# Two-layer diffusion backbone: modulation products with the weights stationary in fp32, and an opening that goes 256 features at a time

## The chip, the cores and the metric

The kernel runs on one core of a Trainium2 chip. The metric is the device time in microseconds (us) of one execution. The engines are named as the profile names them: PE is TensorE (matrix products), PEld its loading of stationary operands, DVE is VectorE, ACT is ScalarE, POOL is GpSimd, and SP issues nearly all transfers.

## What is computed

Two layers act on 1024 latent tokens and 256 context tokens of 1024 features, in fp32. Only the modulation (adaLN) and the opening of the first layer are touched:

```python
def adaln(cond, w_mod, b_mod):                 # w_mod: 1024 x 6144 per layer
    m = jnp.dot(jax.nn.silu(cond), w_mod) + b_mod
    return jnp.split(m[..., None, :], 6, axis=-1)
...
sh1, sc1, g1, sh2, sc2, g2 = adaln(c, w_mod[l], b_mod[l])
csh1, csc1, cg1, csh2, csc2, cg2 = adaln(c_ctx, w_mod[l], b_mod[l])
h = modulate(rms_norm(x, norm1_g[l]), sh1, sc1)
hc = modulate(rms_norm(xc, norm1_g[l]), csh1, csc1)
# ... input projection of h and hc, attention, pooling, convolution, output projection, feed-forward
```

So each layer multiplies two vectors, the conditions of latents and context, by a 1024 x 6144 matrix: 25 MB of weights a layer, for two rows of output. The first layer can't make its first normed tokens before it has two of the six parts, the scale and the shift (chunks 1 and 0).

## The kernel before

Activations lie with features on partitions, 128 features a tile, and tokens along the free axis in blocks of 512, 512 and 256. An exact product of fp32 operands is made of three fast ones: a weight is split into a high and a low part by `Stream.split_to` (ACT copies the high part, DVE or POOL subtracts it), an activation likewise, and `proj` and `proj2` issue hi x hi, hi x lo and lo x hi.

The order of the instructions is written by hand with the help of a forecast. `Clock` keeps a rough time for each engine; work beside the main flow stands in lanes (`lane`, `_step`, `adv`), and a lane's next piece goes out when the forecast says it is due. `fill` gives PE pieces of the lane "ada" before a wait that the forecast sees. Each engine then runs its own instructions in that order.

The modulation before (`adaln`, `adaln_end`): the conditions are the stationary operand, a tile of 128 x 4 (two conditions, high and low parts), and the weights are moving, 512 columns at a time. One half of a chunk is 8 tiles of 128 features; a tile is split on ACT and on POOL (first layer) or DVE (second layer's), and takes two products of 512 columns. The 4 x 512 result is copied by ACT, turned by four transposes into columns, and DVE adds the bias.

- Opening (`run`): the first block's x is loaded, squared on ACT and summed on POOL (`sq_acc`), then all 32 tiles of chunks 1 and 0 (`whole=True`: every other tile unsplit, as two fp32 passes). Only when both chunks are complete does `norm_h` make the first block, feature tile by feature tile (a DVE product, an ACT pass for the high part, a DVE pass for the low one), and `in_proj` multiplies it with the first four column tiles of the input projection (b0, a0, b1, a1). The second block's squares are made during the first block's norm.
- Chunks 2, 4, 3, 5 of the first layer are the lane "ada" beside the rest of the input projection (lower parts on POOL). DVE then has 62 passes of the depthwise convolution over 1009 to 1024 tokens (`taps`) and as many over the context; the pooling's product (`pool_mix`) waits for operands that DVE makes in the same queue.
- All six chunks of the second layer are the lane "ada" beside the first layer's feed-forward.

The sums of squares over the features are themselves products: `rnorm` takes 128 tokens of the squares as stationary fp32 operand and a column of ones (or four of groups) as the moving one.

Of the kernel before, what the change touches and what calls it, by code (L numbers as in the profile page):

```python
# [15 lines left out]
P = 128  # L16
# [14 lines left out]
# column tiles of the input projection, in the order in which they are packed  # L31
# [3 lines left out]
# per-layer parameter columns  # L35
# [13 lines left out]
# when each operation of an attention unit goes out, in the order of which the units' are merged  # L49
# [14 lines left out]
RAW = 10  # L64
SQ = [0, 2, 4, 6, 8, 8, 8, 8, 8]
# [15 lines left out]
class Block:  # L81
    """A run of tokens: its width, and per 128 features the two parts of an operand."""
# [5 lines left out]
class Unit:  # L88
    """128 queries of one head, among the context's tokens or the latents'."""
# [15 lines left out]
class Clock:  # L105
    """A rough forecast of when each engine and each tile is ready, for the order of emission alone."""
# [46 lines left out]
class Eng:  # L153
    """An engine whose instructions are also put to the forecast."""
# [41 lines left out]
class Kern:  # L196
# [57 lines left out]
    def fill(self, *aps):  # L254
        """Before PE has to wait: give it what lanes have for it."""
# [7 lines left out]
    def finish(self, *names):  # L263
        """Emit what is left of lanes now."""
# [6 lines left out]
    def mm(self, out, lhsT, rhs, start, stop):  # L271
        self.tc.nc.tensor.matmul(out, lhsT, rhs, start=start, stop=stop)  # L272
        n = rhs.free_size()
        self.clock.run("pe", n * (0.000422 if rhs.dtype == F32R else 0.00168), [out], [lhsT, rhs] + ([out] if start else []), 0.3)
# [17 lines left out]
    def part(self, shape=(512,), dtype=F32):  # L292
        """Of an operand that stays for the phase."""
# [26 lines left out]
    def split(self, hi, lo, src, lo_eng=None):  # L320
        """hi + lo == src, each of them exact for the tensor engine."""
# [3 lines left out]
    def split2(self, hi, lo, src):  # L325
        """The same on a lane."""
# [41 lines left out]
    def proj(self, hi, lo, blocks, outs, order=range(KD), last=None):  # L368
        """A weight tile's product with some blocks, side by side up to number last."""
# [14 lines left out]
    def proj2(self, ws, blk, outs):  # L384
        """Two tiles' products with one block."""
# [9 lines left out]
    def adaln_setup(self):  # L395
        nc = self.nc
        c4 = self.cp.tile([P, KD, 4], F32, name="cond_raw")
        c_in = self.cp.tile([P, KD, 2], F32, name="cond_in")
        nc.sync.dma_start(c_in, self.io["cond"])
        nc.vector.memset(c4, 0.0)  # L400
        self.S = self.cp.tile([P, KD, 4], F32R, name="cond_st")
        self.c4, c0 = c4, c4[:, :, 0:2]
        self.act(c0, c_in, AF.Silu)
        nc.scalar.copy(self.S[:, :, 0:2], c0)
        nc.vector.tensor_tensor(self.S[:, :, 2:4], c0, r32(self.S[:, :, 0:2]), ALU.subtract)
        self.M = {}

    def adaln(self, l, chunks, pace, ne=2, whole=False, **kw):
# [3 lines left out]
        st = Stream(self, self.mod_aps(l, chunks, ne), new=self.part if whole else self.half if ne == 1 else self.big, **kw)  # L412
        i, ready = 0, []
        for chunk in chunks:
            m = self.cp.tile([P, 2, 8], F32, name=self.name("mod"))
            for n in range(2):
                ps = self.pm.tile([P, 512], F32, tag="mod", name=self.name("mod")) if self.pm else self.bank2()
                for kk in range(KD // ne):
                    if whole:
                        while len(ready) < min(i + 4, len(st.aps)):  # L420
                            w, odd = st.get_raw(len(ready)), len(ready) % 2
                            ready.append((self.part((ne, 512), F32R), self.part((ne, 512), F32R)) if odd else (w, None))
                            if odd:
                                self.split(*ready[-1], w)
                        hi, lo = ready[i]
                    else:
                        hi, lo = st.get(i)
                        yield self.pe(hi, lo, lag=ADA_LAG)
                    i += 1
# [1182 lines left out]
```

## Time and profile before

| | |
|---|---|
| time, median of 3 runs | 3152.94 us (3152.34 to 3154.36) |
| span of the profiled execution | 3148.1 us, 4.8 us under the median |
| PE busy | 2957.6 us, 94% of the span |
| DVE, ACT, POOL busy | 1728.9, 1098.9, 1135.8 us |
| mean granted TensorE clock | 0.977 of full |

The profiled execution took its span and what lies around it; its own time was not listed apart, so the difference to the median, 4.8 us, stands for the start and end that the span leaves out. Times in the rows count from the span's start. A line L272 is the helper that issues every product, L277 the one for transposes, L165 the wrapper of all other instructions, so groups are told apart by their tiles: `mod` is the PSUM bank of the modulation and its result, `cond_st` and `cond_raw` are the conditions, `part` and `half` are small tiles of 512 columns, `big` of 1024, `dww` the convolution's weights, `ones` the column of ones, `bank` a PSUM bank.

### The profile page before, as it was taken

The numbers are of one execution on the slowest core, as the hardware profiler recorded it, in microseconds if no ns is written. First come the engines' busy times: TensorE is split into PE (matmuls) and PEld (weight loads), VectorE is DVE, ScalarE is ACT, GpSimd is POOL, SyncE is SP. The second block draws the span as 40 slices with busy tenths as digits, with TensorE's granted clock in tenths as the row PEclk, the third lists the DMA queues.
The fourth block names the chain that finished last, engine by engine and source line by source line (L and its number), as shares of the span: only waits on it lengthen the run. The fifth ranks groups of instructions, "written<-read, shape, count | busy, mean of one in ns | idle before, by whom it ended". The sixth has DMA issues, their size and how long they took to land.

```text
span 3148.1 us, 38069 instructions
## 1 busy us (share of the span) xinstructions
PE 2957.6 (94%) x14708; PEld 2408.0 (76%) x14708; DVE 1728.9 (55%) x2413; ACT 1098.9 (35%) x1892; POOL 1135.8 (36%) x914
## 2 busy tenths in 40 slices
PE   6868898999999999999999998899999999999999
PEld 2646677877777778888888877678877888888887
DVE  5998758985645454332333498869956222322223
ACT  5424536763423332222222233357744111111110
POOL 3655406871423223233332423318832212211221
PEclk9989898999999999999999999999999999999999
DMA  6324364326333232111111222283252111111111
GB/s 229 108 90 122 123 192 140 105 76 203 114 100 95 93 101 81 34 41 41 34 41 40 75 68 70 81 239 95 88 173 75 48 47 54 47 47 47 48 47 54
DMA packets 133188, 283.52 MB, mean 90 GB/s; under 512 B 13840, under 2 KB 47248, under 8 KB 133008
## 3 DMA queue, kind: packets, MB, share of 16 engines
q1 hardware_dynamic: 132720, 280.83, 28.3%
q8 instruction: 116, 1.90, 0.3%
q14 instruction: 64, 0.52, 0.1%
q10 hardware_dynamic: 288, 0.26, 0.0%
HBM read 231.75 MB, written 49.28 MB: 89 GB/s over the span
## 4 chain that ended last, share of the span: by engine, by line
PE 61%; DVE 8%; issue 2%; ACT 1%; POOL 1%; DMA 1%; SPq 0%; DVEq 0%; ACTq 0%; POOLq 0%
PE bank L272 59%; DVE big L165 4%; DVE st L165 2%; DVE half L165 1%; PE S L272 1%; PE bank L277 1%; DVE part L165 1%; DVE at L165 1%; ACT p L165 0%; ACT big L165 0%; POOL p L165 0%; DMA big<-QS 0%; POOL big L165 0%; ACT half L165 0%; DVE rn L165 0%
## 5 line engine op out<-in xcount | busy, mean ns | idle before, releaser
L272 PE MATMUL bank<-part,big 128*128 128x512 f32 (+1 forms) x7536 | 1625.7, 374 | 29.8 <-DVE part L165 9.0
L272 PEld LDWEIGHTS bank<-part,big 128*128 128x128 f32 x7536 | 1321.6, 191 | 310.3 <-DVE part L165 12.9
L165 POOL TENSOR_TENSOR big<-big,big 128x1024 fp32r<-128x1024 f32 (+2 forms) x177 | 431.7, 2450 | 1141.5 <-ACT big L165 850.0
L272 PE MATMUL bank<-half,big 128*128 128x512 f32 (+1 forms) x2640 | 564.5, 373 | 5.4 <-DVE big L165 2.1
L272 PEld LDWEIGHTS bank<-half,big 128*128 128x128 f32 x2640 | 460.0, 188 | 104.4 <-DVE big L165 4.5
L165 DVE TENSOR_TENSOR big<-big,bank 128x512 f32<-128x512 f32 (+1 forms) x130 | 82.7, 679 | 821.4 <-PE bank L272 450.2
L165 DVE SCALAR_TENSOR_TENSOR big<-bank,mod,big 128x512 f32<-128x512 f32 (+1 forms) x560 | 390.4, 736 | 149.9 <-PE bank L272 143.6
L165 ACT CAST big<-big 128x1024 fp32r<-128x1024 f32 (+2 forms) x322 | 298.4, 955 | 68.8 <-DVE big L165 29.8
L165 POOL TENSOR_TENSOR half<-half,half 128x512 fp32r<-128x512 f32 (+2 forms) x141 | 202.7, 1445 | 328.7 <-ACT half L165 298.3
L165 DVE TENSOR_TENSOR big<-big,big 128x1024 fp32r<-128x1024 f32 (+3 forms) x177 | 214.8, 1220 | 188.1 <-ACT big L165 175.4
L165 ACT ACTIVATE big<-bank 128x512 f32<-128x512 f32 x88 | 48.1, 595 | 607.4 <-PE bank L272 607.4
L165 POOL TENSOR_TENSOR big<-big,half 128x256 f32<-128x256 f32 x160 | 124.7, 780 | 289.4 <-ACT half L165 289.4
L165 POOL TENSOR_TENSOR p<-p,p 128x512 f32<-128x512 f32 (+1 forms) x200 | 221.1, 1105 | 16.7
L165 ACT ACTIVATE half<-bank,mod 128x256 f32<-128x256 f32 x160 | 75.8, 474 | 375.1 <-PE bank L272 375.1
L165 DVE TENSOR_REDUCE st<-S 128x1 f32<-128x1280 f32 (+1 forms) x144 | 195.8, 1362 | 12.3 <-PE S L272 12.3
L165 DVE SCALAR_TENSOR_TENSOR big<-big,dww,big 128x1009 f32<-128x1009 f32 (+14 forms) x120 | 200.2, 1701 | 0.5
L165 POOL TENSOR_SCALAR p<-p,st 128x512 f32<-128x512 f32 (+1 forms) x200 | 123.3, 616 | 192.9 <-DVE st L165 150.7
L165 ACT ACTIVATE p<-S,st 128x1280 f32<-128x1280 f32 (+1 forms) x144 | 177.7, 1234 | 39.7 <-DVE st L165 38.0
L272 PE MATMUL S<-kv,big 128*128 128x512 f32 (+1 forms) x672 | 157.7, 370 | 9.6 <-ACT p L165 6.1
L272 PEld LDWEIGHTS S<-kv,big 128*128 128x128 f32 x672 | 120.1, 191 | 37.7 <-ACT p L165 12.3
L272 PE MATMUL bank<-at,kv 128*128 128x256 f32 x960 | 137.5, 290 | 0.0
L165 DVE TENSOR_TENSOR at<-bank,at 128x512 fp32r<-128x512 f32 (+1 forms) x200 | 115.7, 588 | 29.2 <-ACT at L165 25.0
(107 smaller groups left out, 2364.9 us busy)
## 6 DMA issues: line engine op xcount, KB each, us to landing
big<-in_w_ffn_in SPq DMA_DIRECT2D x88, 512.0 KB, 3.6
big<-in_w_mod SPq DMA_DIRECT2D x48, 512.0 KB, 3.8
big<-in_w_ffn_out SPq DMA_DIRECT2D x44, 512.0 KB, 3.7
big<-in_w_out SPq DMA_DIRECT2D x40, 512.0 KB, 4.9
half<-in_w_mod SPq DMA_DIRECT2D x64, 256.0 KB, 3.5
big<-QS SPq DMA_DIRECT2D x128, 128.0 KB, 5.3
big<-in_w_in SPq DMA_DIRECT2D x28, 512.0 KB, 4.8
VS<-big SPq DMA_DIRECT2D x40, 256.0 KB, 3.6
```

The costliest lines, as they stand in the source:

```text
L165: r = fn(*a, **k)
L272: self.tc.nc.tensor.matmul(out, lhsT, rhs, start=start, stop=stop)
L277: self.tc.nc.tensor.transpose(out, in_, ident)
```

## The change

The weights become the stationary operand, 128 x 128, in fp32 and unsplit, and the two conditions are two moving columns. An item is one chunk's 256 columns: four tiles of 256 rows by 256 columns, 16 products into 2 x 2 columns of PSUM, and DVE adds the bias from there. Copy, transposes and splits of the modulation are gone. The opening goes item by item, shift and scale of 256 features, then two feature tiles of the norm, then the first four column tiles' products with them; the first block's squares aren't summed on POOL any more but by PE (`rnorm` with a list). Comment lines that were taken out are not shown.

```diff
@@ mm
-        self.clock.run("pe", n * (0.000422 if rhs.dtype == F32R else 0.00168), [out], ...
+        self.clock.run("pe", n * 0.000422 if rhs.dtype == F32R else max(0.125, n * 0.00168), [out], ...
@@ rnorm
+        many = s if isinstance(s, list) else [s]
         for c in range(nb):
-            self.mm(ps[:, c * G:(c + 1) * G], s[:, c * P:(c + 1) * P], sel, True, True)
+            for i, x in enumerate(many):
+                self.mm(ps[:, c * G:(c + 1) * G], x[:, c * P:(c + 1) * P], sel, i == 0, i == len(many) - 1)
@@ adaLN
+    def adaln(self, l, items, pace, ne=2, new=None, now=False, raw_ahead=4):
+        st = Stream(self, self.mod_aps(l, items, ne), new=new or self.half, raw_ahead=raw_ahead)
+        n, i = KD // ne, 0
+        for chunk, c in items:
+            ws = []
+            for _ in range(n):
+                ws.append(st.get_raw(i))
+                i += 1
+            yield self.pe(*ws, lag=ADA_LAG)
+            ps = self.pm.tile([P, 512], F32, tag="mod", name=self.name("mod")) if self.pm else self.bank2()
+            for x in range(2):
+                for k in range(KD):
+                    self.mm(ps[:, 2 * x:2 * x + 2], ws[k // ne][:, k % ne, x * P:x * P + P], self.cond[:, k, :], k == 0, k == KD - 1)
+                if not now:
+                    yield pace / 2
+            end = self.adaln_end(l, chunk, c, ps)
+            if now:
+                for _ in end:
+                    pass
+            else:
+                self.lane("mod", end)
+            yield pace / 2
+
+    def adaln_end(self, l, chunk, c, ps):
+        yield self.at(ps)
...
+        nc.vector.tensor_tensor(part, ps[:, 0:4].rearrange("p (c j) -> p j c", j=2), bias, ALU.add)
         if chunk in (1, 4):
...
             nc.vector.scalar_tensor_tensor(part, part, 1.0, g, ALU.add, ALU.mult)
@@ in_proj
         for b in range(n):
+            if opened and b == 0:
+                for x, o in enumerate(opened[1]):
+                    gated(COLS[x], b, o)
+                continue
             self.finish(f"norm{b}")
@@ run
+        nc.sync.dma_start(self.params, io["params"])
+        ada = self.adaln(0, [(ch, c) for c in range(4) for ch in (1, 0)], 0.0, new=self.part, now=True, raw_ahead=4)
...
+        ada_step(1)
...
         for k in range(KD):
             nc.sync.dma_start(xs[k][0], io["xT"][k, :, 0:512])
+            sq.append(self.half())
+            self.act(sq[k], xs[k][0], AF.Square)
+        st_in = self.in_stream(0)
+        st_in.load_to(GATED)
...
+        ada_step(4)
         self.lane("norm0", norm_0())
+        self.finish("norm0")
...
+        ws = [st_in.get(x, 0) for x in range(GATED)]
+        outs = [self.bank() for _ in range(GATED)]
+        for c in range(4):
+            for _ in range(2 if c < 3 else 3):
+                next(norm0, None)
+            if c == 1:
+                for k in range(KD):
+                    nc.sync.dma_start(xs[k][1], io["xT"][k, :, 512:1024])
+            ada_step(4 if c < 3 else 1)
+            for k in range(max(0, 2 * c - 1), 2 * c + 1 if c < 3 else KD):
+                for (hi, lo), o in zip(ws, outs):
+                    self.mm(o, hi[:, k, :], lat[0].hi[k], k == 0, False)
+                    self.mm(o, hi[:, k, :], lat[0].lo[k], False, False)
+                    self.mm(o, lo[:, k, :], lat[0].hi[k], False, k == KD - 1)
...
+        for k in range(KD):
+            self.sq_acc(acc[1], xs[k][1], k == 0)
...
-        self.lane("ada", self.adaln(0, [2, 4, 3, 5], 3.0, ne=1, split_ahead=1, raw_ahead=1, lo=("p",)), ADA_AT)
+        self.lane("ada", self.adaln(0, [(ch, c) for ch in (2, 4, 3, 5) for c in range(4)], 6.0, raw_ahead=1), ADA_AT)
...
-            self.lane("ada", self.adaln(l + 1, [1, 0, 2, 4, 3, 5], 5.0, split_ahead=0, raw_ahead=1))
+            self.lane("ada", self.adaln(l + 1, [(ch, c) for ch in (1, 0, 2, 4, 3, 5) for c in range(4)], 20.0, ne=4, new=self.big, raw_ahead=1))
```

## Rows read from the trace of the kernel before

**Rows 1.** The profile's page: the span, busy time by engine, busy tenths of 40 slices with the granted clock, and the chain of work that ended last.

```profile
span 3148.1 us, 38069 instructions
...
PE 2957.6 (94%) x14708; PEld 2408.0 (76%) x14708; DVE 1728.9 (55%) x2413; ACT 1098.9 (35%) x1892; POOL 1135.8 (36%) x914
...
PE   6868898999999999999999998899999999999999
...
PEclk9989898999999999999999999999999999999999
...
PE 61%; DVE 8%; issue 2%; ACT 1%; POOL 1%; DMA 1%; SPq 0%; DVEq 0%; ACTq 0%; POOLq 0%
```

**Rows 2.** The view by windows, for the stages that hold modulation work and two that hold none (1240 to 1785 the rest of the feed-forward, 1785 to 2060 the second layer's norm and input projection).

```profile
core 0: us, PE busy (x) PEld busy (x) DVE busy (x) ACT busy (x) POOL busy (x), PEclk, DMA share, GB/s
104.00:391.00 287.00, 222.51 (x1079) 168.88 (x1078) 252.49 (x281) 111.35 (x214) 164.89 (x99) 0.88 0.36 118
...
840.00:1240.00 400.00, 397.74 (x2016) 314.53 (x2015) 196.87 (x259) 134.28 (x206) 110.47 (x82) 1.00 0.31 95
1240.00:1785.00 545.00, 545.00 (x2810) 462.92 (x2808) 186.06 (x288) 121.71 (x222) 170.10 (x143) 1.00 0.12 37
1785.00:2060.00 275.00, 239.19 (x1134) 195.44 (x1134) 237.14 (x296) 105.79 (x191) 89.91 (x48) 0.94 0.28 91
```

**Rows 3.** PE's groups of instructions by form: the modulation's products beside the feed-forward and in the first layer, its transposes, and the products with a column of ones, whose stationary operand is 128 x 128 fp32.

```profile
L272 PE MATMUL bank<-big,cond_st 128*4 128x512 f32 x192 | 52.9, 398 | 0.0
L272 PE MATMUL mod<-half,cond_st 128*4 128x512 f32 x128 | 45.6, 418 | 16.2 <-POOL half L165 13.3 <-ACT half L165 2.7
...
L277 PE MATMUL bank<-ident,half 4*128 4x4 f32 x96 | 9.9, 205 | 1.0 <-ACT half L165 0.7 <-ACT rn L165 0.4
L272 PE MATMUL bank<-ones,half 128*128 128x1 f32 x76 | 9.5, 244 | 2.7 <-POOL half L165 2.7
```

**Rows 4.** The timeline (start, length, count): eight records of the four products with ones of one norm at the full clock and what follows them; the loads of the last four such records of another norm at the half clock and what follows; four modulation products in the feed-forward and what follows.

```profile
19.25 0.95 PE L272 MATMUL bank<-ones,half 128*128 128x1 f32 x8
20.13 1.02 PE L272 MATMUL mod<-part,cond_raw 128*4 128x512 f32 x2
...
81.05 0.98 PEld L272 LDWEIGHTS bank<-ones,half 128*128 128x128 f32 x4
81.90 0.33 PEld L272 LDWEIGHTS bank<-part,big 128*128 128x128 f32 x1
...
1101.01 1.11 PE L272 MATMUL bank<-big,cond_st 128*4 128x512 f32 x4
1101.96 2.37 PE L272 MATMUL bank<-half,big 128*128 128x512 f32 x11
```

**Rows 5.** The view by windows (columns as in rows 2), at the start of the attention, where the products are short.

```profile
470.00:475.00 5.00, 4.85 (x20) 4.08 (x19) 2.88 (x10) 3.18 (x12) 2.46 (x5) 0.50 0.47 126
475.00:480.00 5.00, 4.79 (x20) 4.33 (x20) 3.39 (x13) 3.32 (x13) 1.88 (x3) 0.50 1.04 348
```

**Rows 6.** The timeline of the opening: a transfer's issue, first modulation product, POOL's sum of squares, transposes' end and the bias, the first block's first and last products, the second block's first, the end of that block's norm on DVE, and the first result of the second block that DVE takes for the convolution. Then the window of 15 to 29 us.

```profile
5.89 21.64 SPq L165 DMA_DIRECT2D part<-in_w_mod  x32
...
6.61 10.01 POOL L165 TENSOR_TENSOR half<-half,half 128x512 f32<-128x512 f32 x7 [5.31 <-ACT half L165]
...
11.72 1.86 PE L272 MATMUL mod<-part,cond_raw 128*4 128x512 f32 x2 [11.72 <-DMA part<-in_w_mod]
...
42.35 0.41 PE L277 MATMUL bank<-ident,half 4*128 4x4 f32 x4 [0.67 <-ACT half L165]
...
48.11 7.16 PE L272 MATMUL bank<-part,big 128*128 128x512 f32 x19 [5.36 <-ACT part L165]
...
73.75 3.18 PE L272 MATMUL bank<-part,big 128*128 128x512 f32 x13
...
81.97 5.28 PE L272 MATMUL bank<-part,big 128*128 128x512 f32 x12
...
96.78 1.62 DVE L165 SCALAR_TENSOR_TENSOR part<-half,mod,part 128x512 fp32r<-128x512 f32 x2
...
103.92 0.69 DVE L165 SCALAR_TENSOR_TENSOR big<-half,bank 128x512 f32<-128x512 f32 x1 [0.67 <-ACT half L165]
...
15.00:29.00 14.00, 12.86 (x46) 3.13 (x44) 7.25 (x16) 8.00 (x14) 1.61 (x1) 1.00 1.05 387
```

**Rows 7.** POOL's group of the modulation's lower parts from 80 to 391 us; a pass of the convolution by DVE between 104 and 182 us, beside POOL's work, and between 186 and 207 us, with POOL idle; PE's longest wait in the first 400 us (us in total, times, longest) and the product that ended it.

```profile
L165 POOL TENSOR_TENSOR half<-half,half 128x512 fp32r<-128x512 f32 x64 | 108.5, 1712 | 115.6 <-ACT half L165 89.2 <-DVE big L165 7.2 <-ACT rn L165 6.5
...
L165 DVE SCALAR_TENSOR_TENSOR big<-big,dww,big 128x1012 f32<-128x1012 f32 x2 | 4.5, 2240 | 0.0
...
L165 DVE SCALAR_TENSOR_TENSOR big<-big,dww,big 128x1022 f32<-128x1022 f32 x2 | 2.5, 1274 | 0.0
...
PE bank L272 <- DVE big L165: 37.1, 8, 25.8
...
208.97 1.22 PE L272 MATMUL bank<-big,pwr 128*128 128x512 f32 x2 [25.83 <-DVE big L165]
```

**Rows 8.** The timeline: one half chunk's transposes in the first layer, and DVE's reading of their result.

```profile
117.84 0.41 PE L277 MATMUL bank<-ident,half 4*128 4x4 f32 x4
...
127.75 0.15 DVE L165 TENSOR_TENSOR mod<-bank,params 128x8 f32<-128x8 f32 x1
```

More of the change, by code (lines that the diff above doesn't have):

```diff
@@ L63 @@
 P1_LO = ("v", "p", "v") + ("p",) * 11
-RAW = 10
-SQ = [0, 2, 4, 6, 8, 8, 8, 8, 8]
 FFN_LO = ("p",)
@@ L273, in mm @@
         n = rhs.free_size()
-        self.clock.run("pe", n * (0.000422 if rhs.dtype == F32R else 0.00168), [out], [lhsT, rhs] + ([out] if start else []), 0.3)
+        self.clock.run("pe", n * 0.000422 if rhs.dtype == F32R else max(0.125, n * 0.00168), [out], [lhsT, rhs] + ([out] if start else []), 0.3)
     def transpose(self, out, in_, ident):
@@ L406, in adaln_setup @@
-        self.M = {}
-    def adaln(self, l, chunks, pace, ne=2, whole=False, **kw):
-        nc = self.nc
[L412 to L429, printed above, removed]
-                    for e in range(ne):
-                        k = ne * kk + e
-                        if lo is None:
-                            self.mm(ps[0:4], self.c4[:, k, :], hi[:, e, :], k == 0, k == 7)
-                        else:
-                            self.mm(ps[0:4], self.S[:, k, :], hi[:, e, :], k == 0, False)
-                            self.mm(ps[0:4], self.S[:, k, :], lo[:, e, :], False, k == 7)
-                    yield pace * ne / 2
-                m4 = self.half()
-                nc.scalar.copy(m4[0:4], ps[0:4])
-                self.lane("mod", self.adaln_end(l, chunk, n, m4, m))
-        yield 0.0
@@ L443, in adaln_end @@
-    def adaln_end(self, l, chunk, n, m4, m):
-        nc = self.nc
-        yield self.pe(m4)
-        ps = self.bank2()
-        for c in range(4):
-            self.transpose(ps[:, 4 * c:4 * c + 4], m4[0:4, c * P:(c + 1) * P], self.ident[0:4, 0:4])
-        part = m[:, :, 4 * n:4 * n + 4]
-        bias = self.par(l, "bmod", 8 * chunk + 4 * n, 4).unsqueeze(1).to_broadcast([P, 2, 4])
-        for x in (0, 2):
-            nc.vector.tensor_tensor(part, ps[:, 0:16].rearrange("p (c j) -> p j c", j=4)[:, x:x + 2], part if x else bias, ALU.add)
+        self.cond = self.cp.tile([P, KD, 2], F32, name="cond")
@@ L454, in adaln_end @@
+    def adaln_end(self, l, chunk, c, ps):
+        nc = self.nc
+        yield self.at(ps)
+        if (l, chunk) not in self.mods:
+            self.mods[l, chunk] = [self.cp.tile([P, 2, 8], F32, name=self.name("mod")), 0]
+        m, _ = self.mods[l, chunk]
+        part = m[:, :, 2 * c:2 * c + 2]
+        bias = self.par(l, "bmod", 8 * chunk + 2 * c, 2).unsqueeze(1).to_broadcast([P, 2, 2])
+        nc.vector.tensor_tensor(part, ps[:, 0:4].rearrange("p (c j) -> p j c", j=2), bias, ALU.add)
         if chunk in (1, 4):
-            g = self.par(l, "n1g" if chunk == 1 else "n2g", 4 * n, 4).unsqueeze(1).to_broadcast([P, 2, 4])
+            g = self.par(l, "n1g" if chunk == 1 else "n2g", 2 * c, 2).unsqueeze(1).to_broadcast([P, 2, 2])
@@ L465, in mod, with mod_aps @@
         return self.M[l, chunk][:, j, :]
-    def mod_aps(self, l, chunks, ne):
+    def mod_aps(self, l, items, ne):
         w = self.io["w_mod"]
         out = []
-        for ch in chunks:
-            for n in range(2):
-                c0 = ch * D + n * 512
-                for kk in range(KD // ne):
-                    out.append(w[l, kk * ne * P:(kk + 1) * ne * P, c0:c0 + 512].rearrange("(e p) c -> p e c", p=P))
+        for ch, c in items:
+            c0 = ch * D + c * 256
+            for kk in range(KD // ne):
+                out.append(w[l, kk * ne * P:(kk + 1) * ne * P, c0:c0 + 256].rearrange("(e p) c -> p e c", p=P))
         return out
@@ L1265, in run @@
[L1265 to L1267 removed]
+            sq.append(self.half())
+            self.act(sq[k], xs[k][0], AF.Square)
+        st_in = self.in_stream(0)
+        st_in.load_to(GATED)
         rs0 = []
         def norm_0():
[L1271 removed]
+            rs0.append((yield from self.rms(sq)))
+        ada_step(4)
         self.lane("norm0", norm_0())
[L1274 removed]
@@ L1275, in run @@
-        for _ in self.adaln(0, [1, 0], 0.0, ne=1, whole=True, raw_ahead=RAW):
-            self.adv()
-        self.finish("norm0", "mod")
-        lat = [self.new_block(512) for _ in range(2)]
+        self.finish("norm0")
+        del sq
+        lat = [self.new_block(512)]
+        mods = [self.mods[0, ch][0][:, 0, :] for ch in (1, 0)]
+        norm0 = self.norm_h([x[0] for x in xs], rs0[0], mods[0], mods[1], lat[0])
+        ws = [st_in.get(x, 0) for x in range(GATED)]
+        outs = [self.bank() for _ in range(GATED)]
@@ new lines, in run @@
+        acc = [None] + [self.half()[:, :w] for w in (512, CTX)]
+        for c in range(4):
[10 more added lines that the diff above has]
+                    self.mm(o, lo[:, k, :], lat[0].hi[k], False, k == KD - 1)
```

47 lines of the change are left out of this document (18 added, 29 removed).

## The prediction

> **What bounds the kernel now.** I read the page first: PE is busy for 94% of the span and carries 61% of the chain that ended last; the granted clock falls only near slices 1 to 6 and where the layers meet [rows 1]. So the next view was by windows, for the stages that hold modulation work [rows 2]. Three different limits appear. From 840 to 1240 us, in the feed-forward that hosts the second layer's modulation, PE is busy 397.7 of 400 us: whatever PE gets more of there is added to the time. From 104 to 391 us, the input projection with the rest of the first layer's modulation, PE is busy only 222.5 of 287 us, DVE 252.5: a stage bound by DVE as much as by PE. And the opening, up to the second block's first product at 81.97 us, is a chain: loads, modulation, norm, products [rows 6]. The change must be costed in each by itself; the shares of the page can't do it.
>
> **What one product costs, old and new.** The old form puts 512 weight columns through PE. Four of them in the feed-forward take from 1101.01 to 1101.96, 0.24 us each [rows 4]; I take 0.233. The new form has no row, but its twin has: the norms' products with a column of ones also load a 128 x 128 fp32 operand for one moving column. A norm of 512 tokens issues four such products, and the trace shows eight records: each fp32 product is two loads and two passes. Eight records from 19.25 to 20.13 make 0.11 us a record, 0.22 us a product [rows 4]. Bounds: 0.20, and 0.25, which is the group's whole busy time of 9.5 us over 38 products [rows 3]; two columns instead of one should not matter beside a load. At the half clock the four loads from 81.05 to 81.90 are 0.213 us apart, 0.43 us a product [rows 4].
>
> A 256-column item is 16 products: 3.5 us at the full clock, 6.8 at the half one. A chunk is 64 products, 14.1 us, where the old form took 32 of 0.233 = 7.5 us and eight transposes at about 0.085 (0.41 us for four with their tail [rows 6, 8]) = 0.7. So the new form costs PE some 6 us more per chunk. It saves the splits, the copies and the transposes, which are other engines' work except the last.
>
> **Feed-forward (second layer's six chunks).** 384 products x 0.22 = 84.5 us replace 192 x 0.233 = 44.7 [rows 3] and 48 transposes, 4.1. That is +35.7 us, with the bounds 0.20 and 0.25 +28 to +47. The ACT and DVE splits that go were hidden behind a full PE and give nothing. The pace of 20 spreads the items further, but up to 1785 us PE is busy without a gap [rows 2], so no place to hide them comes. Each half item is a burst of 16 records, 1.8 us, between dense products; I expect the clock to stay full there.
>
> **Input projection (four chunks of the first layer).** PE: 256 products x 0.22 = 56.3 against 128 x 0.233 + 32 x 0.085 = 32.5, so +24 us of work. POOL loses 64 subtractions of 1.712 us, 108.5 us in all [rows 7]. That matters to DVE: a convolution pass of 1.27 us with POOL idle takes 2.24 beside POOL [rows 7], so DVE loses 0.97 of every 2.24 us, and 108.5 us x 0.43 = 47 us is the most that comes back. PE's longest wait, 25.8 us at 183 us for a pooling operand that stood behind convolution passes in DVE's queue [rows 7], should go with it. If all of it paid, the stage would be bound by PE: 222.5 + 24 = 247 us instead of 287, -40. But the same stage of the second layer, with no modulation in it, takes 275 us for 239 us of PE and 237 of DVE [rows 2]: about 36 us of waits remain from the chain of norm, pooling and heads, and 247 + 36 = 283 is only -4. DVE's own load falls to about 205 us, lighter than the second layer's 237, so I take -12. On the other side, the result now leaves PSUM by DVE instead of ACT, and there is one bank for it in this phase: the next item on PE waits, with the input projection's products queued behind it, until DVE has come to the bias. DVE was up to 9.5 us late with that (transposes ended 118.26, read at 127.75 [rows 8]). Sixteen items losing 0 to 2 us each would be 0 to 30. Range -40 to +18.
>
> **Opening.** The transfers run at 387 GB/s [rows 6]. In the new order (small ones and items 0 and 1 2.25 MB; x 2.1; four input weights 2.1; items 2 and 3 2.1; two input weights 1.05; items 4 and 5 2.1; second x 2.1; items 6 and 7 2.1) and counting from the old first tile (2.5 MB at 11.72 us), item 0 is there at about 8.4 us, item 1 at 11, x at 16.5, item 7 at 46.5. Before, PE started at 11.72 and ended both chunks at 42.8; the first block's 96 products ran from 48.11 to 76.9 [rows 6].
>
> The question is PE's clock. The new opening begins with nothing but narrow products. At the attention's start PE was covered by records for 4.85 and 4.79 of 5 us, its loads for 4.08 and 4.33, and the granted clock stayed at 0.50, the 1.2 GHz level [rows 5]: records and loads that fill the time don't raise it. The old opening had 512-column passes. So I expect the half clock through the narrow stretches, and again after each group of wide products. Then, in us: item 0 8.4 to 15.2; 0.6 for DVE to empty the one bank; item 1 to 22.6; the sum of squares, now 64 records x 0.213 = 13.6, to 36.2 (before it was 8 records, and 10.0 us of POOL [rows 6] hidden behind the loads); about 2 more to the norm's transposes, 38; items 2 and 3 to 52.5; 12 wide products at the half clock (5.28 us for 12 [rows 6]) to 58; items 4 and 5, one of them perhaps at the full clock, 12, to 70; 24 products, the first 12 of them again as slow as those, 8, to 78; items 6 and 7, 10, to 88; the last 60 products, 16, to 104. That is 27 us later than 76.9. The loads are then no longer the limit (46.5), nor are shorter pieces in them.
>
> The second block's squares now stand behind the first block's norm on ACT, and their sum takes POOL 10 us (the old sum's row [rows 6]), to about 103; then sum product, roots and transposes about 7: its first product at 112 instead of 81.97. The old second block needed 22 us from there to the first result that DVE takes, at 103.92, with DVE's norm still running to 98.4 [rows 6]; the new one has its 16 DVE passes of 0.74 us queued without POOL beside them, 15 us, so 127. The opening costs +23 us. With the full clock the same list gives the 96 products' end at 74, first product of the second block 81, result at 97: -7.
>
> One rule of the Trainium skill speaks otherwise. "TensorE: Matmul & The Clock Gate", section LDWEIGHTS, gives a load's time as its columns over 1.2 GHz, 107 ns for 128, with no word of the clock's level. The rows agree at the full clock (110) and not at the half one (213). By the page alone the narrow items would cost the same at both levels, and the opening would come out near the first rival below.
>
> **Sum.** 3148.1 + 23 (opening) - 12 (input projection) + 35.7 (feed-forward) = 3194.8 us of span; with the 4.8 us between span and median 3199.6. I predict 3200.
>
> **Rivals.**
> - *The clock rises under narrow products.* For it: PE is never idle in the opening's items. Against it: [rows 5]. The opening is then -7: 3148.1 - 7 - 12 + 35.7 + 4.8 = 3170. The same page's section on the clock gate says that it is set by how busy PE has been recently, which could be read this way.
> - *DVE's release pays in full (faster).* The mechanism is POOL's 108.5 us out of DVE's way from 104 to 391 us. The stage goes to -40, and with fewer waits the clock is full in the opening too: 3148.1 - 7 - 40 + 35.7 + 4.8 = 3142. It decides as soon as stage and opening together give back more than 36 us. For it: DVE is busy 252.5 of 287 us and the 25.8 us wait is its doing. Against it: PE's own 247 us and the second layer's waits.
> - *A product is one load, not two.* The change's forecast books 0.125 us for it. Then the feed-forward is 384 x 0.11 - 48.8 = -7, the projection -16, the opening about 0: 3130. Against it: eight records for four products.
> - *The single bank holds PE up (slower still).* DVE's lateness of up to 9.5 us lands on PE 16 times, and narrow bursts at the half clock double: the stage is +18, the opening +28: 3148.1 + 28 + 18 + 36 + 4.8 = 3235. For it: the granted clock is already 0.88 in this stage [rows 2].
>
> **How the numbers follow.** The forecast's case has 0.57, the risen clock 0.15, full payment 0.06, one load 0.04, the bank 0.18. The forecast's own range, from the bounds of its terms, is 3183 to 3220; to leave out no more than 2 in 10 it reaches down to the risen clock and up to the bank: 3163 to 3236. About 0.2%, 6.3 us, is what a measurement of this kernel tells from no change. Faster by more than that needs one of the two fast rivals, 0.09; within it the mixtures between them and the risen clock, 0.04; slower 0.87.
>
> **What would show each step.** Feed-forward: two records of about 0.11 us for each of 384 products, and the stretch to the second layer's norm longer by 36 us. Opening: granted clock 0.5 in the items, loads 0.21 apart, the first wide product near 52, the second block's near 112. Projection: convolution passes near 1.27, no 26 us wait, PE the busier engine; waits of PE on DVE before `mod` products if the bank holds it up. I am wrong if the clock is full by the second item, if a product shows one record, or if the stage from the first convolution pass to the attention shrinks by more than 30 us.

## The result, and the profile after

The changed kernel takes 3190.68 us (median of 4 runs, 3183.08 to 3196.51) against 3152.64 us for the kernel before beside it (4 runs, 3148.14 to 3154.36): ratio 1.0122, 95% interval 1.0104 to 1.0140, slower by 38 us. The profiled execution took 3186.82 us with a span of 3184.8, which is 36.7 us more than the span before. One run of a later kernel, the first under "One part at a time", stands apart from its other three (3776.54 us at a granted clock of 0.72, for 3131.65 to 3133.67) and is left out of that kernel's ratio.

In every execution that lists both, the time is 1.7 to 2.3 us more than the span. The 4.8 us that the forecast added for start and end was therefore in part a difference between two executions of the kernel before: the span forecast, 3194.8, is 10.0 us over the measured one, the time forecast 9.3.

The page, lines of the span, PE and its clock, to be held against [rows 1]:

```profile
span 3184.8 us, 39871 instructions
...
PE 3052.9 (96%) x15820; PEld 2581.9 (81%) x15820; DVE 1583.4 (50%) x2355; ACT 999.1 (31%) x1739; POOL 1016.3 (32%) x843
...
PEclk9889999999999999999999999899999999999999
```

PE has 95 us more work; DVE, ACT and POOL have 146, 100 and 120 us less. The page alone does not say which of these counts where; the windows do. The columns are those of [rows 2], the last row being the stretch of the second layer's norm and input projection:

```profile
104.00:391.00 287.00, 266.79 (x1518) 233.49 (x1517) 219.86 (x319) 92.55 (x175) 70.84 (x46) 0.89 0.39 124
...
840.00:1240.00 400.00, 400.00 (x2230) 346.48 (x2229) 130.23 (x214) 83.69 (x152) 111.34 (x91) 1.00 0.21 68
1240.00:1785.00 545.00, 545.00 (x2976) 469.33 (x2975) 176.81 (x280) 111.99 (x204) 156.62 (x133) 1.00 0.17 56
1785.00:2060.00 275.00, 239.43 (x1120) 196.19 (x1118) 214.16 (x251) 95.13 (x168) 90.98 (x49) 0.92 0.24 81
```

In the first layer's input projection the busier engine has changed: PE 266.8 of 287 us, DVE 219.9 (before 222.5 and 252.5). In the feed-forward PE has no gap left, at the full clock.

The modulation's own records (view by lines and forms of all instructions with the tile `cond`: count, then duration in ns, least, median and most, then first and last start). The three tiles are the three places: `part` the opening, `half` the first layer's lane, `big` the feed-forward.

```profile
L270 PEld LDWEIGHTS bank<-cond,big x768: 187/192/192, 829.7 to 1647.6; 128*128 128x128 f32 x192
...
L270 PEld LDWEIGHTS mod<-cond,half x512: 186/192/338, 130.2 to 379.6; 128*128 128x128 f32 x171
...
L270 PEld LDWEIGHTS mod<-cond,part x256: 186/333/338, 4.4 to 84.9; 128*128 128x128 f32 x128
```

768 records for 384 products: two loads each, as the norms' products had shown [rows 4]. In the feed-forward the load lasts 192 ns at most, in the opening 333 in the median. (One load's length includes its start-up; the spacing is smaller. In the feed-forward a burst of 16 records holds PE for 1.70 us, from 1646.03 to 1647.73, which makes 0.106 us a record and 0.213 a product.)

```profile
1646.03 1.84 PE L270 MATMUL bank<-cond,big 128*128 128x2 f32 x16
1647.73 4.59 PE L270 MATMUL bank<-half,big 128*128 128x512 f32 x22
```

The opening on PE, from the last 20 records of the first item to the second block (timeline: start, length, count, and in brackets the idle time before and its releaser). The item's first 12 records came in groups of four as its weights landed, from 4.44 us.

```profile
8.32 4.43 PE L270 MATMUL mod<-cond,part 128*128 128x2 f32 x20 [0.20 <-DMA part<-in_w_mod]
13.00 6.99 PE L270 MATMUL mod<-cond,part 128*128 128x2 f32 x32 [0.25 <-DVE mod L163]
19.84 13.79 PE L270 MATMUL bank<-ones,half 128*128 128x1 f32 x64
34.81 1.09 PE L275 MATMUL bank<-ident,rn 128*128 128x128 f32 x4 [1.17 <-DVE rn L163]
35.69 6.83 PE L270 MATMUL mod<-cond,part 128*128 128x2 f32 x32
46.45 6.99 PE L270 MATMUL mod<-cond,part 128*128 128x2 f32 x32 [3.93 <-DVE mod L163]
53.30 4.33 PE L270 MATMUL bank<-part,big 128*128 128x512 f32 x12
57.46 3.63 PE L270 MATMUL mod<-cond,part 128*128 128x2 f32 x32
61.35 5.54 PE L270 MATMUL mod<-cond,part 128*128 128x2 f32 x32 [0.26 <-DVE mod L163]
66.75 7.21 PE L270 MATMUL bank<-part,big 128*128 128x512 f32 x24
73.80 4.24 PE L270 MATMUL mod<-cond,part 128*128 128x2 f32 x32
78.30 6.99 PE L270 MATMUL mod<-cond,part 128*128 128x2 f32 x32 [0.25 <-DVE mod L163]
85.14 16.48 PE L270 MATMUL bank<-part,big 128*128 128x512 f32 x60
...
107.15 5.12 PE L270 MATMUL bank<-part,big 128*128 128x512 f32 x13 [2.34 <-ACT part L163]
```

An item of 32 records takes 6.99 us before the first wide products and 3.63 directly behind them. The windows view of three such items says which clock that is:

```profile
13.00:19.80 6.80, 6.80 (x32) 6.80 (x33) 0.14 (x1) 5.78 (x9) 0.00 (x0) 1.00 1.04 407
57.50:61.00 3.50, 3.50 (x33) 3.50 (x31) 0.00 (x0) 0.00 (x0) 0.00 (x0) 1.00 0.00 0
78.50:85.00 6.50, 6.50 (x32) 6.50 (x32) 0.00 (x0) 0.00 (x0) 0.00 (x0) 0.50 0.01 3
```

The last two are as forecast: clock 1.00 and 3.5 us, clock 0.50 and 6.5 us for about the same 32 records. The first has the length of the half clock (1.2 GHz), while its clock column has 1.00. I read the length there, not the column: the item at 13.00 and the one at 78.30, in the row marked 0.50, are the same 32 records and both take 6.99 us. The column stays at 1.00 up to 57 us, whatever the lengths.

**Where the 36.7 us came from.** Times of events in the two profiled executions. The first convolution pass is the first DVE instruction with the tiles `dww,params`, the attention the first PE product into `S`; the feed-forward's start and end are found by counting PE's records without the modulation, the sums and the transposes (the 2,900th and the 7,400th of 12,960). The rows of the first two events, before and after (the attention's with count, least, median and most length in ns, first and last start):

```profile
104.65 1.67 DVE L165 TENSOR_SCALAR big<-big,dww,params 128x1024 f32<-128x1024 f32 x1
121.24 0.81 DVE L163 TENSOR_SCALAR big<-big,dww,params 128x1024 f32<-128x1024 f32 x1
...
L272 PE MATMUL S<-big,big x32: 277/416/582, 463.0 to 482.3; 128*128 128x256 f32 x32
L270 PE MATMUL S<-big,big x32: 274/377/582, 461.7 to 479.4; 128*128 128x256 f32 x32
```

| | before | after | shift | growth of the stretch | forecast |
|---|---|---|---|---|---|
| first convolution pass (opening) | 104.6 | 121.2 | +16.6 | +16.6 | +23 |
| first layer's attention (input projection) | 463.0 | 461.7 | -1.3 | -17.9 | -12 |
| start of the feed-forward | 862.9 | 861.1 | -1.8 | -0.5 | 0 |
| its end | 1792.4 | 1819.5 | +27.1 | +28.9 | +35.7 |
| second layer's attention | 2102.6 | 2140.3 | +37.7 | +10.6 | 0 |
| end of the span | 3148.1 | 3184.8 | +36.7 | -1.0 | 0 |

Three terms have the forecast's sign and about its size. In the stretch up to the attention PE has 28.4 us more work and stands idle 46.3 us less, and the convolution's 124 passes take DVE 33.5 us less (windows of the whole stretch before and after, then DVE's busy time on the tile `dww` alone):

```profile
104.60:463.00 358.40, 293.30 (x1417) 227.41 (x1416) 295.24 (x374) 136.44 (x267) 167.16 (x100) 0.90 0.41 130
121.20:461.70 340.50, 321.73 (x1793) 279.25 (x1792) 247.07 (x387) 105.87 (x208) 69.06 (x42) 0.92 0.44 140
...
104.60:463.00 358.40, 158.41 (x124) 0.90 0.41 130
121.20:461.70 340.50, 124.93 (x124) 0.92 0.44 140
```

The fourth, +10.6 us in a stage that holds no modulation, stood in no step.

### The profile page after: what moved, and what is told of

The parts are those of the page before. It is cut to its first block, busy times and chain, and to the rows that moved or that the text cites. A ratio compares the mean times of both kernels' runs of the same rounds, so it can differ in the third digit from the quotient of the medians.

```text
span 3184.8 us, 39871 instructions
## 1 busy us (share of the span) xinstructions
PE 3052.9 (96%) x15820; PEld 2581.9 (81%) x15820; DVE 1583.4 (50%) x2355; ACT 999.1 (31%) x1739; POOL 1016.3 (32%) x843
## 3 DMA queue, kind: packets, MB, share of 16 engines
q1 hardware_dynamic: 157296, 280.83, 27.7%
## 4 chain that ended last, share of the span: by engine, by line
PE 61%; DVE 9%; issue 2%; ACT 1%; DMA 1%; POOL 0%; SPq 0%; DVEq 0%; ACTq 0%; POOLq 0%
PE bank L270 60%; DVE big L163 4%; DVE st L163 2%; DVE half L163 1%; PE S L270 1%; DVE at L163 1%; PE bank L275 1%; DVE part L163 1%; ACT p L163 0%; DVE rn L163 0%; ACT big L163 0%; DMA big<-QS 0%; ACT at L163 0%; ACT half L163 0%; POOL big L163 0%
## 5 line engine op out<-in xcount | busy, mean ns | idle before, releaser
L163 ACT CAST big<-big 128x1024 fp32r<-128x1024 f32 (+2 forms) x274 | 250.2, 938 | 81.7 <-POOL big L163 39.4
L163 POOL TENSOR_TENSOR big<-big,half 128x256 f32<-128x256 f32 x160 | 118.3, 739 | 291.9 <-ACT half L163 291.9
L163 POOL TENSOR_SCALAR p<-p,st 128x512 f32<-128x512 f32 (+1 forms) x200 | 124.0, 620 | 192.1 <-DVE st L163 148.4
L163 DVE SCALAR_TENSOR_TENSOR big<-big,dww,big 128x1009 f32<-128x1009 f32 (+14 forms) x120 | 180.4, 1534 | 0.5
L163 DVE TENSOR_TENSOR big<-big,big 128x512 fp32r<-128x512 f32 (+3 forms) x129 | 130.6, 1020 | 85.9 <-ACT big L163 78.5
L163 POOL TENSOR_TENSOR half<-half,half 128x512 f32<-128x512 f32 (+1 forms) x70 | 84.8, 1211 | 265.9 <-ACT half L163 263.7
```

What stands on the lines that cost most here:

```text
L163: r = fn(*a, **k)
```

## The experiments

Theory: the feed-forward pays in PE time, the opening in narrow products at the half clock, the first layer's lane gains since POOL stops disturbing DVE, and the rest is the forecast's new price for fp32 products, which changes the order of instructions in places that the change does not name. Rivals: the narrow loads are slow because of the transfers beside them, not the clock; the lane gains from something other than POOL; the second layer's loss is the modulation's late results. Each kernel ran against the kernel before on the same chip. `adaln_w` is the old modulation, kept beside the new one; the new price is in force unless a diff says otherwise. The diffs of the first two kernels are shown against a kernel with every part old and the new price.

**One part at a time.** Only the first layer's lane new (old opening, old lane in the feed-forward):

```diff
-self.lane("ada", self.adaln_w(0, [2, 4, 3, 5], 3.0, ne=1, split_ahead=1, raw_ahead=1, lo=("p",)), ADA_AT)
+self.lane("ada", self.adaln(0, [(ch, c) for ch in (2, 4, 3, 5) for c in range(4)], 6.0, raw_ahead=1), ADA_AT)
```

> The old opening and the old form beside the feed-forward; only chunks 2, 4, 3, 5 of the first layer take the new form. My theory (POOL's 108.5 us out of DVE's way, the 25.8 us wait goes, PE gets 24 us more): the attention begins 12 to 25 us earlier than in the kernel before, time 3128 to 3141. Rival (the gain after the changed opening was only slack that the late opening left to the later engines, the new form itself is worth nothing there): 3150 to 3155.

Measured 3133.33 us, ratio 0.9942 (0.9926 to 0.9959): faster than the kernel before. The attention starts at 436.4, 26.6 us sooner, just over the expectation's 25; by the second layer's attention (2086.8 for 2102.6) 11 of these are lost again.

Only the second layer's lane new:

```diff
-self.lane("ada", self.adaln_w(l + 1, [1, 0, 2, 4, 3, 5], 5.0, split_ahead=0, raw_ahead=1))
+self.lane("ada", self.adaln(l + 1, [(ch, c) for ch in (1, 0, 2, 4, 3, 5) for c in range(4)], 20.0, ne=4, new=self.big, raw_ahead=1))
```

> Only the second layer's six chunks, beside the feed-forward, take the new form. My theory (384 products x 0.22 us on a full PE for 48.8 us of the old): 36 us more than before, 3185 to 3192. Rival (part of the new products falls into gaps that the slower pace reaches, or a product costs one load): 3152 to 3170.

Measured 3196.78 us, ratio 1.0147 (1.0132 to 1.0162), more than expected. The feed-forward itself grows by 27.7 us (870.1 to 1827.3, which is 957.2, for 929.5 before), less than the forecast's 35.7; 7 us were lost before it began and 8 behind it, where nothing of the lane is left. So something else is in this kernel.

Only the opening new; against the changed kernel both lanes are old:

```diff
-self.lane("ada", self.adaln(0, [(ch, c) for ch in (2, 4, 3, 5) for c in range(4)], 6.0, raw_ahead=1), ADA_AT)
+self.lane("ada", self.adaln_w(0, [2, 4, 3, 5], 3.0, ne=1, split_ahead=1, raw_ahead=1, lo=("p",)), ADA_AT)
...
-self.lane("ada", self.adaln(l + 1, [(ch, c) for ch in (1, 0, 2, 4, 3, 5) for c in range(4)], 20.0, ne=4, new=self.big, raw_ahead=1))
+self.lane("ada", self.adaln_w(l + 1, [1, 0, 2, 4, 3, 5], 5.0, split_ahead=0, raw_ahead=1))
```

> Only the opening is new; both lanes keep the old form. My theory (half clock under narrow products): the second block's first product near 107 us as in the changed kernel, instead of 81.97; time 3165 to 3178, since the late start is kept to the end by a stage that DVE still bounds. Rival (the stage behind has slack that takes the delay up): 3150 to 3158.

Measured 3203.39 us, ratio 1.0163 (1.0146 to 1.0180): a miss, +52 where at most 27 was expected. The second block starts at 108.71, as expected, and the first convolution pass comes at 124.0, 19.4 us late, but the attention starts 42.3 us late (505.3). The opening's lateness grows in the stage that follows, where PE waits 51.1 us for DVE's operands (100 to 510 us; 37.1 before, from 100 to 470).

**POOL's share of the lane's gain.** The first kernel again, with 64 subtractions given back to POOL, their results unused:

```diff
             yield self.pe(*ws, lag=ADA_LAG)
+            if l == 0 and not now:
+                for t in ws:
+                    junk = self.half((2, 256), F32R)
+                    self.nc.gpsimd.tensor_tensor(junk, t, t, ALU.subtract)
```

> As the kernel with only the first layer's lane in the new form, but POOL makes 64 subtractions of 512 columns again, one per weight tile, whose results are not used. My theory (the gain of this part is POOL out of DVE's way): most of the gain of 17 us goes, and PE's extra 24 us stay, so 3145 to 3165, with convolution passes of some 2.2 us again. Rival (the gain comes from the waits on the split that are gone, or from the copies off ACT): 3130 to 3138.

Measured 3157.11 us, ratio 1.0031 (1.0019 to 1.0044): the gain in time is gone, and the attention starts at 456.2, 19.8 us later than without the subtractions; of the 26.6 us gained there 6.8 are left. The convolution's passes alone show why (windows view from 104 to 391 us for the tile `dww`; first with POOL free, then with its subtractions):

```profile
104.00:391.00 287.00, 123.13 (x124) 0.92 0.39 126
```

```profile
104.00:391.00 287.00, 146.77 (x124) 0.89 0.36 118
```

The same 124 passes take DVE 23.6 us longer. POOL's work is the cause: nothing waits for its results. (The subtractions do hold the weight tiles longer, so a part of the 20 us at the attention may be that.) The Trainium skill, "GPSIMD Engine Reference", section Specifications, says that POOL shares its SBUF interfaces with DVE and that DVE instructions with two SBUF inputs contend; the convolution's pass is such a one, and this trace agrees.

**The clock in the opening.** The opening kernel, with dummy products of 512 fp32 columns: four before the first item, two in each, four in the sum of squares.

```diff
+    def keep(self):
+        self.mm(self.wide_out, self.ones, self.wide_in, True, True)
@@ run
+        for _ in range(4):
+            self.keep()
@@ adaln, after each 8 products
+                if now:
+                    self.keep()
@@ rnorm, after each group
+            if len(many) > 1:
+                self.keep()
```

> As the kernel with only the opening new, with 512-column fp32 products put in whose result is not used: four before the first item, two in each item, four in the sum of squares; that is 24 x 0.95 us more work for PE at the full clock. My theory (narrow products don't keep the clock up, wide ones do): granted clock 1.0 in most of the opening, narrow loads 0.11 apart, an item 3.5 + 1.9 + 0.6 us instead of 7.5, and the second block's first product at 80 to 92 us instead of 107; time 10 to 20 us under the kernel with only the opening new. Rival (the loads are slow there for another reason, as the transfers beside them): loads stay 0.21 apart and the opening gets 20 to 45 us longer.

Measured 3222.49 us, ratio 1.0229 (1.0214 to 1.0244), 19 us over the kernel without them. As a cure it failed; as a measurement it is clear (timeline of PE):

```profile
3.67 5.21 PE L270 MATMUL bank<-half,ones 128*128 128x512 f32 x8 [3.67 <-DVE half L163]
8.72 1.84 PE L270 MATMUL mod<-cond,part 128*128 128x2 f32 x16
10.42 1.10 PE L270 MATMUL bank<-half,ones 128*128 128x512 f32 x2
11.37 1.84 PE L270 MATMUL mod<-cond,part 128*128 128x2 f32 x16
13.07 1.56 PE L270 MATMUL bank<-half,ones 128*128 128x512 f32 x2
14.43 3.41 PE L270 MATMUL mod<-cond,part 128*128 128x2 f32 x16
```

And the windows of the first and the last of these narrow groups:

```profile
8.70:10.40 1.70, 1.70 (x17) 1.68 (x16) 0.00 (x0) 0.00 (x0) 0.00 (x0) 1.00 1.08 387
14.50:17.60 3.10, 3.10 (x17) 3.10 (x15) 0.00 (x0) 2.92 (x6) 0.00 (x0) 0.50 1.04 402
```

The same 16 records take 1.84 us at clock 1.00 and 3.41 at 0.50, with 387 and 402 GB/s of transfers beside them. The transfers are not what slows them; the clock is. The clock fell although a wide product (two records) stood between each two narrow groups, and the narrow groups stayed at 3.41 us up to the next run of 12 wide products at 66.39. The second block starts at 127.82 instead of 108.71, the 19 us that the whole loses. The Trainium skill, "TensorE: Matmul & The Clock Gate", section LDWEIGHTS, gives a load's time without a word of the clock; these two rows differ by a factor of 1.85, the loads of [rows 4] by 1.9, and the measurement decides.

**The forecast's price.** The kernel before with one line changed, which books time for the order of emission and computes nothing:

```diff
-n * (0.000422 if rhs.dtype == F32R else 0.00168)
+n * 0.000422 if rhs.dtype == F32R else max(0.125, n * 0.00168)
```

> The kernel before with one line changed: the forecast books at least 0.125 us for each fp32 product, as the changed kernel does; the work is the same and only its order moves. In the changed kernel and in each part made alone, the stretch from the end of the feed-forward to the second layer's attention is 6 to 10 us longer than before, though nothing of the modulation is in it. My theory (the new price moves the sums and transposes of the second layer's norm and heads in the order): this kernel shows it too, 3156 to 3163, with the loss between 1790 and 2100 us. Rival (the loss comes from the new form, its buffers or its later lane): 3148 to 3154.

Measured 3162.74 us, ratio 1.0045 (1.0032 to 1.0057). The feed-forward's end is 4.0 us late, the second layer's attention 12.9 (2115.5): between the two this line alone costs 9 us, against the 10.6 of the changed kernel. The rows of that attention, and the windows of the stretch in both kernels:

```profile
L272 PE MATMUL S<-big,big x96: 278/392/504, 2102.6 to 2144.4; 128*128 128x512 f32 x64, 128*128 128x256 f32 x32
L272 PE MATMUL S<-big,big x96: 276/393/505, 2115.5 to 2157.4; 128*128 128x512 f32 x64, 128*128 128x256 f32 x32
...
1792.40:2102.60 310.20, 276.35 (x1308) 226.18 (x1307) 255.34 (x331) 118.50 (x213) 88.88 (x48) 0.95 0.34 107
1796.40:2115.50 319.10, 282.30 (x1308) 230.23 (x1307) 258.52 (x331) 118.56 (x213) 88.70 (x47) 0.93 0.35 110
```

PE has the same 1308 records. They keep it busy 6.0 us longer, at a granted clock of 0.93 for 0.95, and it stands idle 2.9 us longer. Its waits for operands that DVE makes are 4.8 us longer (28.7 for 23.9), other waits shorter. So most of the 9 us is PE's longer busy time at the lower clock; how the new order brings the clock down is not shown.

The other way round: the kernel with the new first lane alone, but with the price of the sums of squares as before, and 0.22 us for the modulation's products (two moving columns). So two prices change at once:

```diff
-max(0.125, n * 0.00168)
+max(0.22 if n == 2 else 0.0, n * 0.00168)
```

> As the kernel with only the first layer's lane in the new form, but the forecast books 0.22 us for a product of the modulation, the measured cost, and for the sums the old price of next to nothing. If the price of the sums is what costs 6 to 10 us in the second layer, this is faster than 3133 by that much: 3122 to 3129. If it isn't: 3130 to 3138.

Measured 3127.49 us, ratio 0.9938 (0.9924 to 0.9951), within the expectation and the fastest kernel of the study. Of the 28 us gained by the attention (435.0) 27 are still there at the second layer's (2075.7), where the first lane kernel had 16 left. Between those two kernels the times are not told apart, as their intervals overlap; the places in the trace are.

The same line, with the same diff, in the changed kernel:

> The changed kernel with the forecast's prices of the run before: 0.22 us for a product of the modulation, next to nothing for the sums. If the price costs the second layer 6 to 10 us, then 3178 to 3186 against 3190.7; if the price is no cause: 3187 to 3195.

Measured 3192.41 us, ratio 1.0138 (1.0124 to 1.0152): a miss, no gain. The stretch between the feed-forward and the second layer's attention grows by 2.1 us instead of 10.6, as expected (the same 1308 records keep PE busy 276.7 us at a clock of 0.95, and 282.5 at 0.93 in the changed kernel); but the order in the first layer changed too, and its attention starts at 474.5 instead of 461.7. The price decides the second layer's loss; it is not a loss that could simply be taken back, since the same line orders the first layer. Which of its two prices moved the first layer is not separated.

**What the first layer's two parts make together.** The changed kernel with the second layer's lane in the old form:

```diff
-self.lane("ada", self.adaln(l + 1, [(ch, c) for ch in (1, 0, 2, 4, 3, 5) for c in range(4)], 20.0, ne=4, new=self.big, raw_ahead=1))
+self.lane("ada", self.adaln_w(l + 1, [1, 0, 2, 4, 3, 5], 5.0, split_ahead=0, raw_ahead=1))
```

> The changed kernel with the second layer's six chunks in the old form (its lane beside the feed-forward as before; the first layer as changed). Theory: the changed kernel's loss of 38 us is the feed-forward's 29 and the 6 to 10 us that the forecast's new price moves in the second layer, and opening and input projection cancel. The new price for the old form's fp32 products stays in place, so part of the second layer's loss stays: 3146 to 3162 us, attention of the first layer starting within 5 us of 462.8. Rival: the parts don't add up (the new opening alone with the old lanes cost 52 us), and the new opening still costs something beside the new lane: 3170 us or more.

Measured 3163.04 us, ratio 1.0040 (1.0025 to 1.0054), one us above the expectation's upper end. The first attention starts at 466.0, 3.0 us late; a further 6 us are lost between the feed-forward and the second layer's attention, where the price alone lost 9.

The same, with the first block's squares summed by POOL again:

```diff
             self.act(sq[k], xs[k][0], AF.Square)
+            if k:
+                nc.gpsimd.tensor_tensor(sq[0], sq[0], sq[k], ALU.add)
...
-            rs0.append((yield from self.rms(sq)))
+            rs0.append((yield from self.rms(sq[0])))
```

> The kernel of the run with the new first layer and the old second one, with the first block's squares summed on GpSimd again and multiplied with ones once (8 records for 64). Theory: at the half clock the 64 records cost 13.8 us on the opening's path, the 8 about 1.7, and GpSimd's sum lies beside the loads: the first block's 96 products end 8 to 13 us sooner (about 90 for 101.6), the second block starts as much sooner, and the whole is 5 to 13 us faster than its twin without this. Rival: the second block waits for its own squares, sum and norm, and the stage behind it has slack, so that the opening's gain is lost by the attention's start: within 3 us of the twin.

Measured 3150.87 us, ratio 1.0002 (0.9991 to 1.0014), 12 us under its twin, whose interval it does not touch. The sum on PE and the second block's first product (timeline; the 64 records take 13.79 us in the changed kernel and in the twin, and the twin's second block starts at 108.10):

```profile
22.68 1.87 PE L270 MATMUL bank<-ones,half 128*128 128x1 f32 x8 [3.12 <-POOL half L163]
...
100.06 20.09 PE L270 MATMUL bank<-part,big 128*128 128x512 f32 x78 [2.33 <-ACT part L163]
```

The first convolution pass comes 9.4 us sooner than in the twin (114.0 for 123.4), the attention 9.0 (457.0), the second layer's 7.8 (2104.2). Most of what the 64 records of the sum cost at the half clock goes through to the end.

## Why the prediction was right

Sign, size and range held: +38 us measured, +47 forecast. By its steps:

- **Opening, +16.6 for +23.** The mechanism was the one named: narrow products at the half clock, item after item, and the sum of squares. The evidence for it was thinner than it looked: [rows 5] hold products of 256 columns, and from 490 to 495 us, in the same attention, the granted clock was 1.00 with PE covered for only 2.91 of 5 us. The list of times came out within 3 us up to the first wide product (53.3 for 52), in part by luck: item 0 ended 2.4 us sooner than listed, and a wait of 3.9 us before item 3, listed as 0.6, took that back. Items 4 to 7 cost 21 us for the 22 listed, two of them mostly at the full clock (3.63 and 4.24 us) and one partly (5.54). The first block's products ended 2.4 us sooner than listed, and the second block followed after 5.5 us instead of 8; these two are most of the 6.4 us by which the term was too dear. The rival of the risen clock fell with the row at 13.00.
- **Input projection, -17.9 for -12.** The 25.8 us wait is gone (the longest left is 3.9, in the row below), the convolution's 124 passes fell from 158.4 to 124.9 us, 33.5 of the 47 us named as the most, and PE became the busier engine, all as said.

```profile
PE bank L270 <- DVE big L163: 8.2, 3, 3.9
```

The size of the gain depends on the opening, which the sum treated as if terms simply add. Attention starts in the four combinations, all at the new price and with the second layer's lane old: old opening 461.2 with the old lane (the kernel with the price alone) and 436.4 with the new; new opening 505.3 and 466.0. The lane is worth 25 us behind the old opening and 39 behind the new one; the opening costs 44 us in front of the old lane and 30 in front of the new one, though the first convolution pass is only 16 to 19 us late. With the new lane the records account for most of the other 14 us: behind the old opening the lane's first 64 records ran before the first convolution pass, 9.1 us of PE's work; behind the new one all 512 come after it (windows of the tile `cond`: PE, PEld and ACT busy, clock, DMA; the kernel with the first lane alone, then the one with the first layer new):

```profile
60.00:107.57 47.57, 9.08 (x64) 9.36 (x64) 0.00 (x0) 0.93 0.28 90
107.57:436.40 328.83, 55.82 (x448) 57.55 (x448) 0.00 (x0) 0.93 0.42 133
...
123.42:466.00 342.58, 63.54 (x512) 65.06 (x512) 0.00 (x0) 0.92 0.43 138
```

For the old lane, where 25 us are added, it was not settled: PE is busy 12 us longer and idle 13 us longer, at a granted clock of 0.87 for 0.90.
- **The single bank.** From 100 to 400 us there is one wait of 5.3 us on DVE before a `mod` product, and in the opening one of 3.9; the rival's sixteen did not come:

```profile
PE mod L270 <- DVE mod L163: 5.3, 1, 5.3
```

- **Feed-forward, +28.9 for +35.7.** The term was mis-sized: a product takes 0.213 us, not 0.22 (384 x 0.213 = 81.8, less 44.7 and 4.1, makes +33.0), and PE's idle 2.3 us of 400 [rows 2] were filled, which I had called no cover. The prediction had read [rows 2] as no gap. The remaining 2 us have no row.
- **The step that was missing.** The diff's first line, the forecast's price, was read only as evidence on the number of loads, and its own effect was priced at nothing without a word. Alone it costs 14 us (3162.74 for 3148.76), 9 of them where the changed kernel lost 10.6. That the total came out within 10 us is in part luck: the three terms together came 19 us too high, and this one, left out, took back more than half of it: -6.4 (opening) - 5.9 (projection) - 6.8 (feed-forward) + 10.6 (price) - 1.5 (elsewhere) = -10.0, which is the difference of the spans, 3184.8 for 3194.8.
- **DVE's release in full (faster).** The mechanism was there, as the run with POOL's subtractions shows, but not the price of 40 us: with the old opening in front the lane brings the attention 27 to 28 us forward and makes the kernel 17 to 21 us faster. And the opening did not get the full clock that this rival asked for. The change holds one part that pays, and two parts and a price that cost more.

## What to carry to other kernels

A product with few moving columns costs its loads: count loads (two for an fp32 operand), not columns, and price them at the clock that such products leave; then ask stage by stage whether PE or another engine sets the time, as the same edit paid beside DVE's convolution and cost beside a full PE. Where DVE sets the time, work taken off POOL is worth what it frees on DVE; work moved from POOL to PE, like the sum of squares here, costs what PE needs for it at the clock of that place (13.79 us). In a kernel whose order is planned by a forecast, a changed price is a change of the order everywhere: give it a run of its own before the rest is judged.

## What had not been expected

One 512-column product between each two groups of 16 narrow records did not hold the clock up: two groups took 1.84 us, the third and the following ones up to the next wide run 3.41, at a granted clock of 0.50. In the opening the clock column reads 1.00 where the records have the length of the half clock (an item of 6.99 us at 1.00 and another of 6.99 at 0.50): at the start of a span a record's length is the better witness. And a line that computes nothing moved the time by 0.45%, most of it where the same records ran at a lower clock.
